# One core, one layer of RetNet + S5: tokens in natural order, modulation products with the weights stationary, and the S5 eigenvalues computed in the head

## The chip, the cores and the metric

The kernel runs on one core of one Trainium2 chip. The metric is the device time of one execution in microseconds (us), and the time before is the median of three runs. A core has five engines that each follow a queue of their own: TensorE (PE, with the weight loads counted apart as PEld), VectorE (DVE), ScalarE (ACT), GpSimd (POOL) and SyncE (SP), which here only issues DMA transfers; sixteen DMA engines carry these.

## The reference

One layer of a decoder over a prompt of 2048 tokens and eight short sample sequences (8 x 8 tokens), with 1024 channels, all in float32. Nine rows of conditioning `c` (one for the prompt, eight for the samples) become six modulation vectors each:

```
mod = silu(c) @ w_ada + b_ada                       # 9 x 6144
sh1, sc1, gt1, sh2, sc2, gt2 = split(mod, 6)
h = rms_norm(x, norm1_g) * (1 + sc1) + sh1
q, k, v, g, u, gate_r, gate_s = split(h @ w_in, ...)
q, k = rotary(q, pos), rotary(k, pos) * 128**-0.5
ret = rms_normalize(retention(q, k, v)) * silu(g)   # 4 heads, chunks of 128
lam_bar = exp((lam_re + i lam_im) * exp(log_dt))    # 32 groups x 64 states
b_bar = (lam_bar - 1) / lam * b
ssm = gelu(s5(u, lam_bar, b_bar, c, d))             # a linear recurrence over tokens
ssm = ssm * sigmoid(ssm @ w_glu)
merged = sigmoid(gate_r) * (ret @ w_br) + sigmoid(gate_s) * (ssm @ w_bs)
x = x + gt1 * (merged @ w_out)
h2 = rms_norm(x, norm2_g) * (1 + sc2) + sh2
x = x + gt2 * (square(relu(h2 @ w_up)) @ w_down)
y = rms_norm(x, norm_f_g)
```

The last states of the retention and of S5 are outputs too.

## The kernel before

**Stages.** A head (`setup`) prepares the modulation that the first normalization needs, and the first 512 rows of x. Then four super-blocks of 512 prompt tokens each (`super_block`, b = 0 to 3; b = 1 carries the sample tokens with it) run the mixer, and `feed_forward` runs the MLP and stores the rows of y.

**Products.** A dense product is split in three: an operand is written as a rounded part (hi, type fp32r) and the rest (lo), and hi*hi, hi*lo and lo*hi are summed in PSUM. Weights come in units of 128 x 2 x 512 float32 (512 KB): SyncE loads `wraw` (`fetch`, L181), ScalarE copies out `whi` (L191), and GpSimd, or VectorE for some names, subtracts to get `wlo` (L194, in `refill`). Four raw units and five split ones are buffered; `plan` fixes the order of the whole stream. A block (`block`, L253) takes four units (u, q, k, v, g, the four gate halves gr0, gs0, gr1, gs1, and wo0, wo1) or two (glu, br, bs). For each unit PE runs four groups of six products with 512 columns, one group for each of four PSUM banks. The results in the banks are evacuated behind the last unit: u by ScalarE (`ue`, L1528, which reorders tokens for S5 and is stored to DRAM), q and k by VectorE with the rotary factors (`rt`, L1555 to L1557), v by VectorE, g and the gates by ScalarE.

**Fillers.** Everything else is a generator (a filler): S5, retention, the norm of the next super-block, the output. `tick`, called once behind each group of six products, counts the fillers down and lets those due issue their next step, up to their next `yield n`. So the place of a filler's instructions in each engine's queue is set by the numbers in its `yield`s and by the delay it was spawned with; `finish(f)` issues the rest of one. Scheduling is otherwise the program's order, in which the compiler moves instructions a little.

**Modulation.** The 6144 columns of `w_ada` are twelve blocks of 512. Blocks 0 to 3 (sh1 and sc1) are computed in the head: `wa` holds a block as two halves of 1 MB, eight in all, and each block is eight float32 products in which the nine conditioning rows `z` are stationary and 512 weight columns move (L849), giving 9 x 512. Blocks 4 to 11 lie in super-block 0, one behind each of its first eight dense blocks (`more_ada`): their weights are in the ring's stream like any other (`names` "ada4" to "ada11", whose lo part is always VectorE's), and sixteen products with 512 columns (L259) give hi and lo sums in rows 0 to 8 and 32 to 40, which `ada`'s `evac` adds to the bias (L906, L907). In both cases the 9 x 512 sum is transposed back by four small PE products (L887 in the head, L913 later) into `modT`, 128 channels x 48 x 9. Blocks 4, 5, 10 and 11 also go to DRAM as rows (`modd`), where gt1 and gt2 are read across tokens.

**S5 setup.** `s5_setup` is a generator: loads of lam, dt, b, c, d; the eigenvalue part (L982 to L1077: expm1, sine and cosine by polynomials, all on 128 x 32 or 128 x 64 elements, on VectorE); powers by doubling (L1099 on); and sixteen groups of products that fold b and c with the powers into tables in DRAM (`s5bx`, `pw` L1155, `pk` L1156, `s5c`). It is spawned before u of super-block 0, and `finish(s5)` before v issues what is left of it; S5 proper (`s5`) runs beside v and g.

**Rows of tokens.** Inside each 128 tokens the kernel works in the order tau(r) = 8 (r mod 16) + r div 16. `x_rows` (L1450) loads rows with a pattern of three levels for that, the stores of y (L529 and `output_rows`) write with the same one, and the constants (causal mask, decay, rotary tables) follow it. S5 works on eight phases of the token index: with this order the eight phases of 16 tokens lie in runs of 16, which `ue` and `gw` (L1627) move as runs.

The functions that the change touches, with the lines as the profile numbers them:

Of the kernel before, what the change touches and what calls it, by code (L numbers as in the profile page):

```python
# [10 lines left out]
F32 = mybir.dt.float32  # L11
# [29 lines left out]
def _constants():  # L41
# [7 lines left out]
    tau = 8 * (r % 16) + r // 16  # L49
# [19 lines left out]
    pos = np.arange(SB)  # L69
    tok = 128 * (pos // 128) + 8 * (pos % 16) + pos % 128 // 16  # L70
# [12 lines left out]
class Layer:  # L83
# [79 lines left out]
    def plan(self, names, sides):  # L163
        self.names = list(names)
        self.stream = []
        for n, queue in zip(names, sides):
            for v in self.views(n):
                self.stream.append((n, v))
                if queue and n[:2] not in ("ad", "wo"):
                    self.stream.append(queue.pop(0))  # L170
# [5 lines left out]
        self.at = 0  # L176
# [8 lines left out]
    def refill(self, keep=False):  # L185
        nc = self.nc
        if self.split < len(self.stream):
# [5 lines left out]
            eng = nc.vector if name == "ad" or name in SIDE and self.split % 4 < 2 else nc.gpsimd  # L193
# [41 lines left out]
    def block(self, name, kind, src, evac=None, sample=None, order="k"):  # L235
# [5 lines left out]
        banks = [self.pd.tile([P, 512], F32, tag="pd", name=f"pd_{name}") for _ in range(4)] if kind else []  # L241
# [20 lines left out]
        if order == "k":  # L262
            for u in range(nu):
                w = self.weight(name)
                for j in range(4 if kind else 0):
# [7 lines left out]
                if sample:  # L273
                    for kk in range(2):
                        sample_products(2 * u + kk, w, kk)
                    if u == nu - 1:
                        self.spawn(sample[1](sb))
                    if kind is None:
                        self.refills()
                        self.tick()  # L280
                self.due += 1
                self.side()
            return
# [193 lines left out]
    def turn_back(self, k, g, i, accs):  # L477
# [44 lines left out]
        for t in range(4):  # L522
            for n in range(4):
# [5 lines left out]
                nc.sync.dma_start(raw_ap(self.o[0], P * (t0 + t) * D + 256 * n, [[D, 8], [8 * D, 16], [1, 256]]), o)  # L529

    def output_rows(self):
# [6 lines left out]
        for t in range(10):  # L538
# [3 lines left out]
            if t > 1:  # L542
# [3 lines left out]
                nc.sync.dma_start(raw_ap(self.o[0], P * (t - 2) * D, [[D, 8], [8 * D, 16], [1, D]]), o)  # L546
# [134 lines left out]
    def norm_out(self, pt, q, s, b, hh, hl, j, eng):  # L681
        nc = self.nc
        m = self.work("m", [P, 4, P])
        for a in range(4):
            k = 4 * q + a
            if eng is nc.vector:
                nc.scalar.activation(m[:, a], pt[:, a], AF.Identity, scale=s[:, k:k + 1], bias=b[:, k:k + 1])
            else:
                nc.vector.tensor_scalar(m[:, a], pt[:, a], s[:, k:k + 1], b[:, k:k + 1], op0=ALU.mult, op1=ALU.add)
# [82 lines left out]
    def setup(self):  # L772
# [24 lines left out]
        self.gT = cst.tile([P, 2, 8], F32, name="gT")  # L797
        self.R = cst.tile([P, H, P], F32, name="R")
        self.rk = cst.tile([P, 8], F32, name="rk")
        self.cT = cst.tile([P, 8, 41], F32R, name="cT")  # L800
        gn = self.work("gn", [16, P])
        dma(gn[0:8], i["norm1_g"].rearrange("o (k p) -> (o k) p", p=P))
        dma(gn[8:16], i["norm2_g"].rearrange("o (k p) -> (o k) p", p=P))
# [8 lines left out]
        ba = self.unit("ba", shape=(9, 2048))  # L812
        load(0)
        self.x_rows(xu[0][:, 0], 0, 0)
        dma(ba, raw_ap(i["b_ada"], 0, [[0, 9], [1, 2048]]))
        self.x_rows(xu[0][:, 1], 0, 1)
        load(2)
        for j in range(2, 4):
            self.x_rows(xu[1][:, j - 2], 0, j)
        load(1)  # L820
        load(3)
        for _ in range(RAW):
# [5 lines left out]
        V.tensor_scalar(th, th, 0.5, None, op0=ALU.mult)  # L828
# [3 lines left out]
        pg = self.bank("pg", [P, 16])  # L832
        nc.tensor.transpose(pg, gn, self.ident[:16, :16])
        z = self.unit("z", shape=(P, 8, 41))
        V.memset(z, 0.0)
        V.tensor_copy(self.cT, z)
        V.tensor_copy(z[:, :, 0:9], pt)
        nc.scalar.activation(self.cT[:, :, 0:9], z[:, :, 0:9], AF.Copy)
        V.tensor_sub(self.cT[:, :, 32:41], z[:, :, 0:9], self.cT[:, :, 0:9])
        V.tensor_copy(self.gT.rearrange("p a k -> p (a k)"), pg)  # L840
# [3 lines left out]
        x = [xu[j // 2][:, j % 2] for j in range(4)]  # L844

        def ada(n):
            pa = self.pd.tile([P, 512], F32, tag="pd", name=f"ps_ada{n}")
            for k in range(8):
                nc.tensor.matmul(pa[:9], z[:, k, 0:9], wa[2 * n + k // 4][:, k % 4], start=(k == 0), stop=(k == 7))  # L849
            self.mod_out(n, pa[0:9], ba[:, 512 * n:512 * n + 512])  # L850
# [8 lines left out]
        for q in range(2):  # L859
            ada(q)  # L860
            if q == 0:
                for j in range(4):
                    r = self.now(self.row_rstd(x[j]))
                    V.tensor_scalar(x[j], x[j], r, None, op0=ALU.mult)
                pts = [turn(q, j) for j in range(4)]
            else:
                for _ in range(2):
                    self.refill(True)
            ada(2 + q)
            self.scales(2 + q)  # L870
            for j in range(4):
                pt = turn(q, j) if q else pts[j]
                self.norm_out(pt, q, self.s1[:, :, 0], self.modT[:, 0:8, 0], self.hh, self.hl, j, nc.gpsimd)
        for _ in range(RING - 2):
            self.refill(True)
        self.late_setup = self.s5_setup()
        next(self.late_setup)

    def mod_out(self, n, p, bias):
        nc = self.nc  # L880
        t = self.work("mt", [9, 512])
        nc.vector.tensor_add(t, p, bias)
        if n in (4, 5, 10, 11):
            nc.sync.dma_start(self.modd[:, 512 * n:512 * n + 512], t)
        pt = self.pd.tile([P, 4, 9], F32, tag="pd", name="ptm")
        for a in range(4):
            nc.tensor.transpose(pt[:, a], t[:, a * P:a * P + P], self.ident[:9, :9])  # L887
# [944 lines left out]
```

## Time and profile before

| | |
|---|---|
| median of three runs | 3103.24 us (3094.15 to 3113.18) |
| the profiled execution's own time | 3099.62 us |
| its span in the trace | 3097.8 us |
| mean granted TensorE clock | 0.967 of full speed |
| busy: PE, PEld | 2911.6 us (94%), 2378.3 us (77%) |
| busy: DVE, ACT, POOL | 1822.8 us (59%), 1407.0 us (45%), 1720.4 us (56%) |
| moved by DMA | 518.62 MB, a mean of 167 GB/s |

Times in the trace count from the span's start. A group "L253 PE MATMUL pd_u<-hh,whi 128\*128 128x512" is line 253's products from `hh` and `whi` into bank `pd_u`, the stationary operand's shape ahead of the moving one's; "xN" is the number of records and the figure after the time is the duration, or the mean. A float32 product leaves two records. "idle <-X" names what released the engine. PE's ends are modelled, and the clock is the share of full speed granted by the throttle in that stretch.

### The profile page before, as it was taken

The page shows a single profiled execution, that of the slowest core. Times are in us where ns is not written, and L with a number is a line of the kernel's source. Part 1 is how long each engine was busy: PE and PEld are TensorE (multiplying, and loading weights), DVE is VectorE, ACT ScalarE, POOL GpSimd, SP SyncE. Part 2 cuts the span into 40 slices and gives each one's busy share as a digit, 9 for nine tenths or more (in the row PEclk, how much of TensorE's full clock was granted, in tenths as well). Part 3 has the DMA queues.
Part 4 walks back from the last instruction along what each step waited for, and adds up shares of the span by engine and source line. Part 5 has one row for each costly group of instructions (what it writes and reads, how often), then busy time and mean ns, then how long its engine had stood idle before and what let it go on. Part 6 is the DMA issues. An engine that isn't in the chain of part 4 may idle for free. (4 is left out here: it accounts for less than half of the span.)

```text
span 3097.8 us, 37373 instructions
## 1 busy us (share of the span) xinstructions
PE 2911.6 (94%) x13436; PEld 2378.3 (77%) x13436; DVE 1822.8 (59%) x2937; ACT 1407.0 (45%) x2296; POOL 1720.4 (56%) x1036
## 2 busy tenths in 40 slices
PE   7789999999999899999999989999999999998996
PEld 3567787788777778877788778887888788877875
DVE  5978644770575786365842545555556755554655
ACT  2233463322353334534234345566655555566743
POOL 2331464435253644655445477668777666688771
PEclk9889999999999999999999999999999999999998
DMA  8466445643236954447544455556545544466532
GB/s 231 156 192 209 132 128 165 185 110 119 80 92 191 277 181 121 141 137 245 190 133 151 148 191 180 187 197 204 186 154 171 193 168 155 150 220 225 182 128 96
DMA packets 336749, 518.62 MB, mean 167 GB/s; under 512 B 71462, under 2 KB 168246, under 8 KB 332459
## 3 DMA queue, kind: packets, MB, share of 16 engines
q1 hardware_dynamic: 336564, 516.23, 52.6%
q8 instruction: 106, 1.74, 0.2%
q14 instruction: 79, 0.65, 0.1%
HBM read 401.39 MB, written 114.78 MB: 167 GB/s over the span
## 5 line engine op out<-in xcount | busy, mean ns | idle before, releaser
L194 POOL TENSOR_TENSOR wlo<-wraw,whi 128x1024 fp32r<-128x1024 f32 x248 | 616.8, 2498 | 729.0 <-ACT whi L191 585.7
L409 PE MATMUL pq_down<-shi,tw 128*128 128x512 f32 x1792 | 565.5, 395 | 20.7 <-DVE acc L469 10.2
L191 ACT ACTIVATE whi<-wraw 128x1024 fp32r<-128x1024 f32 x312 | 324.4, 1058 | 571.2 <-PE pd_wo L253 63.7
L409 PE MATMUL pq_up<-shi,tw 128*128 128x512 f32 x1792 | 556.9, 391 | 11.9 <-ACT tw L310 8.0
L409 PEld LDWEIGHTS pq_down<-shi,tw 128*128 128x128 f32 x1792 | 340.2, 190 | 96.1 <-ACT acc L467 10.4
L409 PEld LDWEIGHTS pq_up<-shi,tw 128*128 128x128 f32 x1792 | 337.6, 188 | 84.9 <-ACT tw L310 9.2
L311 POOL TENSOR_TENSOR tw<-traw,tw 128x512 fp32r<-128x512 f32 x192 | 274.4, 1442 | 144.7 <-ACT tw L310 144.4
L409 PE MATMUL pq_down<-slo,tw 128*128 128x512 f32 x896 | 353.1, 394 | 0.9 <-DVE slo L382 0.9
L409 PE MATMUL pq_up<-slo,tw 128*128 128x512 f32 x896 | 349.7, 391 | 0.0
L396 ACT ACTIVATE shi<-sw 128x1024 fp32r<-128x1024 f32 x140 | 147.0, 1057 | 167.4 <-DMA sw<-sd 107.9
L469 DVE SCALAR_TENSOR_TENSOR acc<-pq_down,modT,acc 128x512 f32<-128x512 f32 x224 | 161.9, 745 | 95.3 <-PE pq_down L409 95.0
L409 PEld LDWEIGHTS pq_down<-slo,tw 128*128 128x128 f32 x896 | 170.5, 190 | 36.0 <-DVE slo L382 1.4
L409 PEld LDWEIGHTS pq_up<-slo,tw 128*128 128x128 f32 x896 | 168.9, 189 | 34.5
L382 DVE TENSOR_TENSOR slo<-sw,far 128x512 fp32r<-128x512 f32 x160 | 103.7, 682 | 113.3 <-ACT far L381 99.6
L310 ACT ACTIVATE tw<-traw 128x512 fp32r<-128x512 f32 x224 | 137.4, 624 | 54.7 <-PE pq_down L409 39.1
L401 DVE TENSOR_TENSOR slo<-sw,shi 128x1024 fp32r<-128x1024 f32 x60 | 117.7, 1976 | 71.8 <-ACT shi L396 70.6
L419 ACT ACTIVATE aq<-pq_up 128x512 f32<-128x512 f32 x128 | 72.6, 592 | 170.7 <-PE pq_up L409 170.7
L194 DVE TENSOR_TENSOR wlo<-wraw,whi 128x1024 fp32r<-128x1024 f32 x64 | 88.3, 1380 | 73.0 <-ACT whi L191 68.6
L345 POOL TENSOR_TENSOR ts<-traw,ts 128x512 f32<-128x512 f32 x64 | 95.2, 1487 | 53.9 <-issue 49.2
L253 PE MATMUL pd_wo<-whi,mh 128*128 128x512 f32 x256 | 103.9, 410 | 18.9 <-DVE tw L1718 18.9
L310 ACT ACTIVATE tw<-ts 128x512 fp32r<-128x512 f32 x128 | 80.2, 627 | 81.2 <-PE pq_up L409 71.9
L311 POOL TENSOR_TENSOR tw<-t,tw 128x512 fp32r<-128x512 f32 x64 | 88.4, 1387 | 50.2 <-ACT tw L310 50.2
(537 smaller groups left out, 6865.4 us busy)
## 6 DMA issues: line engine op xcount, KB each, us to landing
wraw<-in_w_in_dram SPq DMA_DIRECT2D x144, 512.0 KB
sw<-sd SPq DMA_DIRECT2D x112, 512.0 KB
s5p<-s5c SPq DMA_DIRECT2D x32, 1024.0 KB
traw<-in_w_up_dram SPq DMA_DIRECT2D x64, 512.0 KB
sd<-sq SPq DMA_DIRECT2D x32, 1024.0 KB
sd<-aq SPq DMA_DIRECT2D x32, 768.0 KB
traw<-in_w_down_dram SPq DMA_DIRECT2D x24, 1024.0 KB
wraw<-in_w_ada_dram SPq DMA_DIRECT2D x32, 512.0 KB
```

The costliest lines, as they stand in the source:

```text
L191: a = nc.scalar.activation(hi, raw, AF.Copy)
L194: l = eng.tensor_sub(lo, raw, hi)
L253: nc.tensor.matmul(banks[j], a, b, start=(k == 0 and z == 0), stop=(k == nk - 1 and z == 2))
L310: self.nc.scalar.activation(t[:, 0], x, AF.Copy)
L311: eng.tensor_sub(t[:, 1], x, t[:, 0])
L345: G.tensor_sub(x[p], l, x[m] if isinstance(m, int) else m)
L382: self.nc.vector.tensor_sub(d, a, c)
L396: nc.scalar.activation(hi[:, a], t, AF.Copy)
L401: V.tensor_sub(lo[:, a], t, hi[:, a])
L409: self.nc.tensor.matmul(bank, w, x, start=(first and a == 0 and z == 0), stop=(a == 3 and z == 2), skip_group_check=True)
L419: copy = lambda d, b: nc.scalar.activation(d, b, AF.Copy)
L469: V.scalar_tensor_tensor(d, b, g, d, op0=ALU.mult, op1=ALU.add)
```

## The change

Three things change.

*Token order.* Tokens keep their natural order inside 128 rows. Loads and stores of rows become plain two-level patterns; the constants follow; the reorder for S5 in `ue` and `gw` now reads or writes every eighth element.

*Modulation.* In all twelve blocks the weights become the stationary operand, 128 x 128 float32 at a time, and the nine columns of `z` move, so the sums come out with the channels across partitions, where `modT` wants them. In the head that makes 128 small products in place of 32. Bias and gains are loaded as 64 rows and transposed once (`bg`). Blocks 4 to 11 leave the ring's stream: `ada_fetch` loads one unit of raw weights into a buffer of two (`wada`), and `ada_side`, called behind each unit of a dense block of super-block 0 (32 times), asks for the next unit, issues eight small products and spawns the one addition that folds them into `modT`. Only blocks 4, 5, 10 and 11 are transposed back (`pr`) for `modd`. `norm_out` scales on ScalarE always, and so does the head's `norm`.

*S5 setup.* The eigenvalue part runs in the head, in four pieces (`next(s5)`); the loads of b, c, d and the transposes of c come later; the pauses between the steps change; `first_s5` chains the remainder with S5 proper, which is finished behind gr0 instead of before retention. Retention of super-block 0 therefore begins behind gr0, not before it.

The order of instructions on PE in the head, up to the first products of u (one row for a run of like instructions; `pt` are transposes of x and of the conditioning, `ptm` those of the sums). Before:

```order
L831 MATMUL pt<-cpk,th 128x9 x8
L833 MATMUL pg<-cpk,gn 128x16
L849 MATMUL ps_ada_176<-wa,z 9x512 x8
L887 MATMUL ptm<-cpk,mt 128x9 x4
L849 MATMUL ps_ada_285<-wa,z 9x512 x8
L856 MATMUL pt<-cpk,x_125 128x128 x8
L887 MATMUL ptm<-cpk,mt 128x9 x4
L849 MATMUL ps_ada_332<-wa,z 9x512 x8
L856 MATMUL pt<-cpk,x_126 128x128 x8
```

Afterwards (`pl` are the transposes of lam for S5):

```order
L829 MATMUL pt<-cpk,th 128x9 x8
L831 MATMUL pg<-cpk,gb 128x64
L843 MATMUL ps_ada<-z,wa 128x9 x32
L982 MATMUL pl<-cpk,lam 128x32 x2
L862 MATMUL pt<-cpk,x_126 128x128 x4
L843 MATMUL ps_ada<-z,wa 128x9 x2
L862 MATMUL pt<-cpk,x_126 128x128 x4
L843 MATMUL ps_ada<-z,wa 128x9 x60
L862 MATMUL pt<-cpk,x_127 128x128 x4
```

Each block's eight wide products became thirty-two narrow ones, the `ptm` transposes are gone, and two for S5 have come in.

The order on PE behind u in super-block 0. Before, one modulation block stands between the last products of u and the first of q:

```order
L253 MATMUL pd_u<-hh,wlo 128x512
L259 MATMUL ps_ada_816<-whi,cT 41x512
L259 MATMUL ps_ada_816<-wlo,cT 41x512
L259 MATMUL ps_ada_816<-whi,cT 41x512
L259 MATMUL ps_ada_816<-wlo,cT 41x512
L259 MATMUL ps_ada_816<-whi,cT 41x512
```

Afterwards, a burst of eight stands among the products of u, behind its first unit:

```order
L252 MATMUL pd_u<-hh,wlo 128x512
L252 MATMUL pd_u<-hh,whi 128x512 x4
L918 MATMUL ps_ada<-z,wada 128x9 x8
L252 MATMUL pd_u<-hl,whi 128x512 x4
L252 MATMUL pd_u<-hh,wlo 128x512
```

The sixteen products in a row are replaced by bursts of eight, each behind one unit of a dense block.

The order on VectorE at the end of the head. Before, the eigenvalue steps (`s5w`) stand behind the last modulation sum:

```order
L888 COPY modT<-ptm 128x36
L894 TENSOR_SCALAR s_108<-modT 128x36
L895 TENSOR_TENSOR s_108<-s_108,gT 128x36
L689 TENSOR_SCALAR m<-pt,s_108,modT 128x128 x16
L982 TENSOR_SCALAR s5w<-s5w 128x32
L983 TENSOR_SCALAR s5w<-s5w 128x32
```

Afterwards they stand ahead of the second modulation sum of the head (block 2's), up to line 1068:

```order
L1067 TENSOR_TENSOR s5w<-s5w 128x32
L1068 TENSOR_SCALAR s5w<-s5w 64x32
L849 TENSOR_TENSOR modT<-ps_ada,bg 128x36
L850 TENSOR_TENSOR modT<-modT,ps_ada 128x36
L946 TENSOR_SCALAR s_108<-modT 128x36
L947 TENSOR_TENSOR s_108<-s_108,bg 128x36
```

The scalings of x by `norm_out` (L689) have left VectorE's queue.

The diff, cut to its core:

```diff
-    tau = 8 * (r % 16) + r // 16
+    tau = r
...
-    tok = 128 * (pos // 128) + 8 * (pos % 16) + pos % 128 // 16
+    tok = np.arange(SB)
...
                 self.due += 1
                 self.side()
+                self.ada_side()
...
-                nc.sync.dma_start(raw_ap(self.o[0], P * (t0 + t) * D + 256 * n, [[D, 8], [8 * D, 16], [1, 256]]), o)
+                nc.sync.dma_start(raw_ap(self.o[0], P * (t0 + t) * D + 256 * n, [[D, P], [1, 256]]), o)
...
-                nc.tensor.matmul(pa[:9], z[:, k, 0:9], wa[2 * n + k // 4][:, k % 4], ...)
+        def products(n):
+            pa = self.pd.tile([P, 2, 4, 9], F32, tag="pd", name="ps_ada")
+            for h in range(2):
+                for a in range(4):
+                    for k in range(4):
+                        nc.tensor.matmul(pa[:, h, a], wa[2 * n + h][:, k, a * P:a * P + P], z[:, 4 * h + k],
+                                         start=(k == 0), stop=(k == 3))
+        def sums(n, pa):
+            m = self.modT[:, 4 * n:4 * n + 4]
+            V.tensor_add(m, pa[:, 0], self.bT[:, 4 * n:4 * n + 4, None].to_broadcast([P, 4, 9]))
+            V.tensor_add(m, m, pa[:, 1])
...
+        pa = products(0)
+        norm(0)
+        sums(0, pa)
+        next(s5)
+        norm(1)
+        pts = [turn(0, 0), turn(0, 1)]
+        pa = products(2)
+        sums(2, pa)
...
+    def ada_fetch(self, at):
+        if at < 32:
+            self.nc.sync.dma_start(self.ada_w[:, at % 2], self.ada_todo[at][2])
+    def ada_side(self):
...
+        w = self.ada_w[:, at % 2]
+        self.ada_fetch(at + 1)
+        p = self.bank("ps_ada", [P, 4, 9])
+        for a in range(4):
+            for k in range(2):
+                nc.tensor.matmul(p[:, a], w[:, k, a * P:a * P + P], self.z[:, 2 * u + k], ...)
+        def evac():
+            yield 1
+            nc.vector.tensor_add(m, p, m if u else self.bT[...])
...
-    def ada(self, n):
...
+    def first_s5(self):
+        yield from self.late_setup
+        yield 6
+        yield from self.s5(0, 4)
...
-            nc.scalar.activation(t.rearrange("p (s n c) -> p n s c", s=8, n=4),
-                                 p.rearrange("p (n s c) -> p n s c", s=8, n=4), AF.Copy)
+            nc.scalar.activation(t.rearrange("p (s c) -> p s c", s=8), p.rearrange("p (c s) -> p s c", s=8), AF.Copy)
...
-    src = raw_ap(self.i["x_prompt"], (b * SB + P * j) * D, [[D, 8], [8 * D, 16], [1, D]])
+    src = raw_ap(self.i["x_prompt"], (b * SB + P * j) * D, [[D, P], [1, D]])
...
-        if b == 0:
-            self.finish(s5)
-            s5 = self.spawn(self.s5(b, 4), 13)
...
             self.block(n, "T", srcT(hh, hl), ev_gate(n), S(hS, ev_gS(a)))
-            more_ada()
+            if not b and a == 0:
+                self.finish(s5)
+                rh, rl = begin()
```

More of the change, by code (lines that the diff above doesn't have):

```diff
@@ L168, in plan @@
                 self.stream.append((n, v))
-                if queue and n[:2] not in ("ad", "wo"):
+                if queue and n[:2] != "wo":
                     self.stream.append(queue.pop(0))
@@ L192, in refill @@
             name = self.stream[self.split][0][:2]
-            eng = nc.vector if name == "ad" or name in SIDE and self.split % 4 < 2 else nc.gpsimd
+            eng = nc.vector if name in SIDE and self.split % 4 < 2 else nc.gpsimd
             l = eng.tensor_sub(lo, raw, hi)
@@ L264, in block @@
                 w = self.weight(name)
-                for j in range(4 if kind else 0):
+                for j in range(4):
                     for kk in range(2):
@@ L857, in turn, with out @@
             return pt
[L859 to L873, printed above, removed]
+        def out(pt, q, j):
+            self.norm_out(pt, q, self.s1[:, :, 0], self.modT[:, 0:8, 0], self.hh, self.hl, j, nc.gpsimd)
@@ new lines, in setup @@
+        pa = products(0)
+        norm(0)
+        sums(0, pa)
+        next(s5)
+        norm(1)
+        pts = [turn(0, 0), turn(0, 1)]
+        pa = products(2)
+        sums(2, pa)
+        for j in range(2):
+            out(pts[j], 0, j)
+        next(s5)
+        for j in range(2, 4):
+            norm(j)
+        for j in range(2, 4):
+            out(turn(0, j), 0, j)
+        for _ in range(2):
+            self.refill(True)
+        next(s5)
+        pa = products(1)
+        sums(1, pa)
@@ L874, in setup @@
+        pts = [turn(1, j) for j in range(4)]
+        pa = products(3)
+        sums(3, pa)
+        for j in range(4):
+            out(pts[j], 1, j)
         for _ in range(RING - 2):
             self.refill(True)
-        self.late_setup = self.s5_setup()
-        next(self.late_setup)
-    def mod_out(self, n, p, bias):
-        nc = self.nc
[L881 to L885, printed above, removed]
-        for a in range(4):
-            nc.tensor.transpose(pt[:, a], t[:, a * P:a * P + P], self.ident[:9, :9])
-        nc.vector.tensor_copy(self.modT[:, 4 * n:4 * n + 4], pt)
+        next(s5)
@@ L1476, in run @@
         names, sides = [], []
-        late = iter(range(4, 12))
         for b in range(NSB):
-            main = []
-            for n in ("u", "q", "k", "v", "g", "gr0", "gs0", "gr1", "gs1"):
-                main.append(n)
-                if b == 0 and n != "gs1":
-                    main.append(f"ada{next(late)}")
+            main = ["u", "q", "k", "v", "g", "gr0", "gs0", "gr1", "gs1"]
             main += ["glu", "br0", "br1", "bs0", "bs1", "wo0", "wo1"]
@@ L1494, in run @@
         self.setup()
-        late = iter(range(4, 12))
         for b in range(NSB):
-            self.super_block(b, late)
+            self.super_block(b)
         self.finish(*self.fillers)
```

199 lines of the change are left out of this document (96 added, 103 removed).

## The prediction

> **What bounds the kernel now.** I read the page first, then busy time by stage (columns after the length: busy us and instructions of PE, PEld, DVE, ACT, POOL; then PE's granted clock, the DMA share, GB/s), then who PE waits for.
>
> ```profile
> PE 2911.6 (94%) x13436; PEld 2378.3 (77%) x13436; DVE 1822.8 (59%) x2937; ACT 1407.0 (45%) x2296; POOL 1720.4 (56%) x1036
> ```
>
> ```profile
> 0.00:57.90 57.90, 39.32 (x121) 11.69 (x121) 21.44 (x76) 12.36 (x25) 10.29 (x10) 0.94 0.86 256
> 57.90:85.20 27.30, 27.30 (x124) 20.85 (x123) 26.52 (x95) 13.81 (x19) 12.31 (x7) 1.00 0.78 183
> 85.20:163.80 78.60, 60.46 (x269) 46.71 (x269) 77.33 (x171) 21.18 (x23) 29.92 (x15) 0.87 0.44 137
> 163.80:205.20 41.40, 29.41 (x129) 23.51 (x128) 40.26 (x54) 9.78 (x16) 14.89 (x8) 0.90 0.64 215
> 205.20:214.90 9.70, 9.33 (x48) 9.23 (x48) 5.49 (x13) 2.39 (x4) 0.00 (x0) 0.50 0.32 129
> 214.90:310.20 95.30, 89.36 (x494) 74.01 (x495) 74.67 (x171) 31.94 (x52) 18.89 (x8) 0.95 0.70 212
> 310.20:516.50 206.30, 199.29 (x922) 160.12 (x921) 113.02 (x184) 95.77 (x156) 101.64 (x49) 0.97 0.44 135
> ```
>
> ```profile
> PE pd_k L253 <- DVE rt L1556: 10.2, 1, 10.2
> PE pw L1155 <- DVE s5bx L1148: 8.0, 1, 8.0
> PE pt L913 <- DVE mt L907: 7.9, 1, 7.9
> PE pd_v L253 <- DVE rt L1556: 3.7, 1, 3.7
> ```
>
> PE is the bound: 94% of the span. The head lasts until 57.9 us, super-block 0 from there to 516.5 (458.6 us). Only in the head and in super-block 0 does another engine set the pace: from 57.9 to 205.2 VectorE is busy 144.1 of 147.3 us, and PE's four longest waits there, 29.8 us together, are on VectorE. The waits also cost clock: 0.87, 0.90 and 0.50. The compiled order of super-blocks 1 to 3 is nearly the old one and that of the feed-forward part is the old one on PE, so the sum is made over the head, super-block 0, and the loads and stores of token rows.
>
> **The head: S5 eigenvalues.** Inside super-block 0 these small VectorE operations meet ScalarE and GpSimd at work; in the head GpSimd does nothing until 42 us.
>
> ```profile
> 84.58 2.43 DVE L1032 TENSOR_SCALAR s5w<-s5w 128x64 f32<-128x64 f32 x1
> ...
> 94.08 0.18 DVE L1032 TENSOR_SCALAR s5w<-s5w 128x64 f32<-128x64 f32 x1
> ```
>
> ```profile
> 82.74 11.34 POOL L194 TENSOR_TENSOR wlo<-wraw,whi 128x1024 fp32r<-128x1024 f32 x4 [12.00 <-ACT whi L191]
> ```
>
> The same operation costs 0.18 us alone and 2.43 us while GpSimd runs a split. Some 130 of them leave super-block 0; at 0.18 they are 23 us in the head, on an engine that has 36 us free there (57.9 - 21.44). They stand ahead of the second modulation sum in VectorE's queue, but need PE only for one early pair of transposes, and PE will be later than they (next part): nothing on the path. If PE were quick there, they would hold that sum back a few us. The head's 32 scalings of x move from VectorE to ScalarE (busy 12.36 of 57.9 us): the last 16 and their copies, estimated at 0.3 to 0.6 us each from ue's 0.6 us for 512 columns (below), take 7 to 12 us, and PE spends 11 us on the first half of u meanwhile (48 products at 0.23): nothing.
>
> **The head: modulation products.** Before, 32 float32 products with 512 moving columns, two records each; afterwards 128 with 9 moving columns and a float32 block of 128x128 to be loaded for each. The nearest rows to these are the S5 products with 16 moving columns, at both clocks, and those with 64.
>
> ```profile
> 9.90 8.53 PE L849 MATMUL ps_ada<-wa,z 128*9 128x512 f32 x16 [1.25 <-DVE z L837]
> 24.56 9.73 PE L849 MATMUL ps_ada<-wa,z 128*9 128x512 f32 x16 [4.95 <-DMA wa<-in_w_ada_dram]
> 34.22 1.41 PE L856 MATMUL pt<-cpk,x 128*128 128x128 f32 x8
> 49.77 7.04 PE L849 MATMUL ps_ada<-wa,z 128*9 128x512 f32 x16
> ...
> 192.19 0.96 PE L1156 MATMUL pk<-s5bc,s5bx 128*128 128x16 f32 x8
> 210.36 1.73 PE L1156 MATMUL pk<-s5bc,s5bx 128*128 128x16 f32 x8
> 211.93 1.09 PE L1155 MATMUL pw<-cpk,s5bx 128*128 128x128 f32 x4
> ```
>
> ```profile
> 1503.89 0.33 PE L1242 MATMUL py<-s5t,s5p 128*128 128x64 f32 x2
> ...
> 1505.40 0.39 PE L1241 MATMUL py<-s5u,s5p 128*128 128x64 f32 x2
> 1505.91 0.39 PE L253 MATMUL pd_v<-whi,hl 128*128 128x512 f32 x1
> ```
>
> At full clock seven py products take 1.51 us (1503.89 to 1505.40), 0.22 each, and four pk at most 0.96, 0.24 each: I take 0.22; the columns hardly enter. At half clock four pk take 1.57 us (210.36 to 211.93), 0.39 each, a transpose at most 0.27 (1.09 / 4). Which clock will it be? From 205.2 to 214.9 PE was busy 9.33 of 9.70 us and PEld 9.23, with these small products, and the clock stayed at 0.50 throughout. A stream of 9 columns is thinner still, so I take half clock for the whole head: 128 x 0.39 = 50 us and 32 transposes x 0.25 = 8, from 9.9: PE reaches u at 68, not 57.9: **+10**. A lower bound: the 48 records from 205.2 to 214.9 are 16 pairs of a transpose and a pk, 0.61 a pair, so 0.36 for pk, and u at 63: +5. u then begins cold; the product that began cold took 9.73 us against 7.04, so **+3**. Weights are no limit: eight tiles of 1 MB, four x tiles and two weight pieces of half a MB, 11.5 MB, land at 50 us even at the head's 256 GB/s of now, ahead of the last 32 products.
>
> [...]
>
> **Super-block 0, what goes.** The eight late modulation blocks of 16 products, their transposes and their VectorE work:
>
> ```profile
> 81.58 0.39 PE L259 MATMUL ps_ada<-whi,cT 128*41 128x512 f32 x1
> 85.25 0.40 PE L253 MATMUL pd_q<-hh,whi 128*128 128x512 f32 x1
> ```
>
> ```profile
> L194 DVE TENSOR_TENSOR wlo<-wraw,whi 128x1024 fp32r<-128x1024 f32 x32 | 42.2, 1318 | 21.2 <-ACT whi L191 21.2
> L913 PE MATMUL pt<-cpk,mt 9*128 9x9 f32 x32 | 3.6, 214 | 7.9 <-DVE mt L907 7.9
> ```
>
> PE gives back 8 x 3.67 (81.58 to 85.25) = 29.4 us and 3.6 of transposes. VectorE loses 42 us of splits and the eigenvalues, and gains 32 small additions, so it no longer fills 57.9 to 205.2: the 29.8 us of waits go, and with them the lost clock, 60.46 x 0.13 + 29.41 x 0.10 + 9.33 x 0.50 = 15.5. Together **-78.3**.
>
> **Super-block 0, what comes.** 256 products with 9 columns in bursts of eight. Between dense products the clock stays full (the dense product at 1505.91, behind the py run, takes 0.39, the full-clock duration), so 256 x 0.22 = 56.3 us, all on PE's path (at 0.24: 61). Sixteen transposes at 0.18 (34.22): 2.8. What is late next: PE itself, and S5's chain on VectorE, which now lies in gr0 and gs0; I leave 8 us of waits (0 to 20). In seven places of the order bursts stand beside S5 or retention products, so that 4 to 7 us pass without a dense product; such a run can lose the clock as at 205.2, 2.7 us each: five of seven, 13.5 (0 to 19). Together **+80.6**. The block ends **+2**: its PE work grew by what its waits shrank. Retention begins a gate block later and still has three blocks to lie beside.
>
> **Token rows.** The old strided patterns run at half the DMA engines. At the end, where nothing else runs:
>
> ```profile
> 3085.00:3090.00 5.00, 0.00 (x0) 0.00 (x0) 0.00 (x0) 0.00 (x0) 0.00 (x0) 0.50 0.54 190
> ```
>
> ```profile
> 3071.49 22.51 SPq L529 DMA_DIRECT2D out_dram<-acc  x32
> 80.65 0.37 SPq L181 DMA_DIRECT2D wraw<-in_w_in_dram  x1
> ```
>
> Share 0.54 at 190 GB/s; the plain weight loads reach a share of 0.86 with these mixed in. 32 stores leave SyncE 0.70 us apart, a plain one is issued in 0.37. The last 16 wait for a norm that is ready at 3080.6; at 0.45 each they are out at 3088 and land at 3090, not 3097.8. Between -2 (issue stays at 0.6) and -8 I take **-6**. The 28 row loads and 8 stores elsewhere are hidden but share the engines with weights: **-3** (0 to -6).
>
> In exchange the reordering for S5 now reads or writes every eighth element:
>
> ```profile
> L1528 ACT ACTIVATE ue<-pd_u x16: 577/602/639, 79.9 to 1414.0; 128x512 f32<-128x512 f32 x16
> ```
>
> ```profile
> 95.20 0.17 DVE L1062 COPY cs<-s5w 128x32 f32<-128x32 f32 x1
> ...
> 107.01 0.20 DVE L1099 COPY s5pw<-s5pw 128x32 f32<-128x32 f32 x1
> ```
>
> VectorE copies every eighth of 32 elements (L1099) in 0.20 us, contiguous ones (L1062) in 0.17. I take 0 for the 32 ScalarE operations; at twice the time, +0.6 each, only the four before q and the four before glu are near the path: 5 us a super-block at the most, 20 in all if nothing covered them. [...]
>
> **The sum.** +10 +3 +2 -6 -3 = +6 us, against the profiled execution's own 3099.62 (span 3097.8): 3105.6. The median of the runs is 3103.24, 3.6 us above that execution, so I forecast 3109 as a median, 0.2% up. Its own range, with the terms at their bounds and taken as independent (root of the squares): downwards 5 (head), 8 (waits), 13.5 (clock), 2 and 3 (rows) make 17; upwards 12 (waits), 5.5 (clock), 5 (products), 4 and 3 (rows) and 10 (half of the strided copies) make 18: 3092 to 3127.
>
> **Rivals.** [...] 14%.
>
> *PE waits for the late weights.* The late modulation weights now come in a two-slot buffer straight to PE, asked for one quarter block (7 us) ahead, in SyncE's queue behind loads, S5 tables and ue stores that wait for others. Now ScalarE meets them, nine pieces ahead of use:
>
> ```profile
> ACT whi L191 <- DMA wraw<-in_w_ada_dram: 24.1, 9, 9.4
> ```
>
> If those nine waits fell on PE: +24, and five cold starts, 13.5: 3146, slower by 1.4%. Behind such a wait stand the block's dense products, and behind those the evacuations of u, q, k, v. It decides where a load takes over 7 us from its turn. For it: DMA share 0.78 in u, and S5's small loads. Against: 0.44 to 0.64 from q on. 14%.
>
> *Every burst drops the clock.* 32 x 2.7 = 86, less 13.5: 3182. The py burst of the same length did not. 4%.
>
> *The change saves no PE work and no waits matter* (VectorE's relief comes to nothing, as the waits move to S5's steps in gr0): the 29.8 and 15.5 stay, less the 8 left above, +37: 3146. Against: the 42 us of splits and the eigenvalues that leave. 6%.
>
> **How the numbers follow.** Likeliest 62%. 1% is 31 us and about what a measurement of this kernel tells from no change. Below 3072: most of the first rival's 14%, less what falls just short: 0.09. Above 3134: the other rivals, 24%, of which some fall short, and little of the likeliest: 0.18. Within: 0.73. The range takes in half of the first rival and most of the second: 3076 to 3146.
>
> **What would show it.** Right: u's first product at 63 to 70 us with the clock at 0.5 before it; ps_ada records at about 0.2 us a record in the head and 0.11 later; no wait of PE on rt between 85 and 205; super-block 1 beginning near 530; the last store landing 20 us after PE's end. Wrong: u beginning before 50 (the first rival), PE waits on wada (the second), ps_ada followed by dense products 0.43 us apart (the third), ue over 1 us.

## The result

The changed kernel takes 3067.43 us (median of four runs, 3065.49 to 3075.05). The kernel before, run beside it, takes 3101.14. The ratio is 0.9882, with a 95% interval of 0.9856 to 0.9908: 1.2% faster. The forecast was 3109 us with a range of 3076 to 3146, so the time lies outside the range and on the other side of no change.

The head and super-block 0 went as forecast. On the timeline of TensorE in the changed kernel (start, length, line, tiles, count), u begins at 66.84 us; the forecast said 68. The small products take 13.79 us for 64 records, two a product, 0.43 us each:

```profile
8.71 13.79 PE L843 MATMUL ps_ada<-z,wa 128*128 128x9 f32 x64 [0.70 <-DMA wa<-in_w_ada_dram]
...
25.29 25.61 PE L843 MATMUL ps_ada<-z,wa 128*128 128x9 f32 x120
...
66.84 0.77 PE L252 MATMUL pd_u<-hh,whi 128*128 128x512 f32 x1
```

Super-block 1 begins at 530.8, and "near 530" was the forecast. Everything behind that was forecast 9 us shorter and is 45 us shorter. The table gives the lengths of the stages in the two profiled executions, and in two experiments told of below. A stage ends where the next one's first product starts; the last two columns are split at TensorE's last product. Executions of the same instructions differ by 2 or 3 us in most stages, and by 7 in super-block 2, which took 401.4 and 402.7 us in two runs and 408.7 and 409.3 in two others whose edits lie outside it.

| us | head | super-block 0 | 1 | 2 | 3 | feed-forward | tail |
|---|---|---|---|---|---|---|---|
| before | 57.9 | 458.5 | 458.3 | 412.8 | 404.0 | 1281.1 | 25.1 |
| changed | 66.8 | 463.9 | 445.9 | 401.4 | 400.9 | 1269.4 | 18.6 |
| token order alone | 47.1 | 454.7 | 449.8 | 402.8 | 400.8 | 1272.7 | 18.9 |
| the other two alone | 70.8 | 467.3 | 457.2 | 409.8 | 408.7 | 1279.7 | 25.3 |

Busy time hides this. The page's first line says that TensorE is now busy longer, not less:

```profile
PE 2949.6 (96%) x13980; PEld 2467.9 (80%) x13980; DVE 1741.1 (57%) x2873; ACT 1395.4 (45%) x2295; POOL 1723.8 (56%) x1036
```

The waits of TensorE from super-block 1 on say where to look. Of the kernel before, from 516 to 1790 us (waiting tile and who is waited for, total, times, longest), the first row is the one that matters:

```profile
PE pd_wo L253 <- DVE tw L1718: 16.2, 4, 6.4
```

In the changed kernel it is

```profile
PE pd_wo L252 <- DVE tw L1739: 2.4, 1, 2.4
```

Block wo's banks are emptied by VectorE's `tw`, the product of the sum and gt1. In super-block 1 of the kernel before, the timelines of SyncE and VectorE show the load of gt1 issued behind the four loads of x, and the first `tw` 19.7 us later:

```profile
924.00 2.68 SPq L1450 DMA_DIRECT2D x<-in_x_prompt_dram  x4
926.73 0.49 SPq L926 DMA_DIRECT2D gt<-modd  x1
```

```profile
946.44 0.69 DVE L1718 SCALAR_TENSOR_TENSOR tw<-pd_wo,gt 128x512 f32<-128x512 f32 x1 [16.64 <-DMA gt<-modd]
```

In the changed kernel the order of the loads is the same, and 8.2 us pass:

```profile
935.18 0.63 SPq L954 DMA_DIRECT2D gt<-modd  x1
```

```profile
943.39 0.69 DVE L1739 SCALAR_TENSOR_TENSOR tw<-pd_wo,gt 128x512 f32<-128x512 f32 x1 [4.34 <-DMA gt<-modd]
```

The busy time by stretches (last three columns: granted clock, DMA share, GB/s) shows why. Where little but the old pattern's rows is under way (936 to 944 us), the mean busy share of the DMA engines is 0.51 to 0.52, and 131 to 132 GB/s move; with the plain pattern the share reaches 1.03, and 411 GB/s move. Before, then after:

```profile
936.00:940.00 4.00, 4.00 (x20) 3.30 (x19) 0.00 (x0) 0.73 (x1) 0.00 (x0) 1.00 0.52 131
```

```profile
937.00:941.00 4.00, 4.00 (x13) 3.21 (x14) 0.69 (x1) 0.60 (x1) 0.00 (x0) 0.57 1.03 411
```

The slowest dimension of the old pattern has 8 entries, that of the plain one 128. Why the one is carried at half the share of the other isn't shown.

For block wo of super-block 1 as a whole (before, then after), 7.2 us went and the mean clock rose from 0.92 to 0.97: the waits had cost clock too.

```profile
909.40:974.80 65.40, 55.42 (x230) 44.93 (x230) 31.84 (x33) 14.44 (x20) 22.06 (x11) 0.92 0.45 131
```

```profile
918.50:976.70 58.20, 53.20 (x231) 43.53 (x229) 33.57 (x33) 14.36 (x20) 23.07 (x11) 0.97 0.44 146
```

The tail was forecast 6 us shorter and is 6.5 shorter. The 32 stores leave SyncE in 17.44 us, not 22.51, and the last norm, ready at 3056.23, is followed by 10.7 us, not 17.2:

```profile
3047.12 17.44 SPq L526 DMA_DIRECT2D out_dram<-acc  x32
...
3056.23 3.30 ACT L525 ACTIVATE acc<-acc,y 128x256 f32<-128x256 f32 x8 [3.55 <-DVE y L631]
```

### The profile page after: what moved, and what is told of

It reads as the page before. It is cut to its first block, busy times and chain, and to the rows that moved or that the text cites. A ratio compares the mean times of both kernels' runs of the same rounds, so it can differ in the third digit from the quotient of the medians.

```text
span 3067.0 us, 38337 instructions
## 1 busy us (share of the span) xinstructions
PE 2949.6 (96%) x13980; PEld 2467.9 (80%) x13980; DVE 1741.1 (57%) x2873; ACT 1395.4 (45%) x2295; POOL 1723.8 (56%) x1036
## 4 chain that ended last, share of the span: by engine, by line
PE 75%; DVE 12%; DMA 5%; ACT 3%; issue 2%; POOL 2%; SPq 1%; ACTq 0%; DVEq 0%; POOLq 0%
PE pq_up L406 17%; PE pq_down L406 14%; PE pd_gr L252 6%; PE pd_gs L252 5%; PE pd_wo L252 4%; PE pd_br L252 3%; PE pd_g L252 3%; PE pd_u L252 3%; DMA sw<-sd 2%; PE pd_k L252 2%; PE ps_ada L843 2%; PE pd_bs L252 2%; PE ps_ada L918 2%; PE pd_glu L252 2%; PE pd_q L252 1%
## 5 line engine op out<-in xcount | busy, mean ns | idle before, releaser
L406 PE MATMUL pq_up<-shi,tw 128*128 128x512 f32 x1792 | 557.1, 391 | 10.8 <-ACT tw L307 6.9
L190 ACT ACTIVATE whi<-wraw 128x1024 fp32r<-128x1024 f32 x280 | 291.9, 1060 | 564.5 <-issue 56.1
L307 ACT ACTIVATE tw<-ts 128x512 fp32r<-128x512 f32 x128 | 80.2, 627 | 80.9 <-PE pq_up L406 71.6
L342 POOL TENSOR_TENSOR ts<-traw 128x512 f32<-128x512 f32 x64 | 86.8, 1357 | 45.1 <-DMA traw<-in_w_up_dram 26.8
L444 DVE TENSOR_TENSOR sq<-aq 128x512 f32<-128x512 f32 x32 | 30.5, 952 | 131.4 <-ACT aq L421 131.4
```

The source lines that it names most:

```text
L190: a = nc.scalar.activation(hi, raw, AF.Copy)
L307: self.nc.scalar.activation(t[:, 0], x, AF.Copy)
L342: G.tensor_sub(x[p], l, x[m] if isinstance(m, int) else m)
L406: self.nc.tensor.matmul(bank, w, x, start=(first and a == 0 and z == 0), stop=(a == 3 and z == 2), skip_group_check=True)
```

## The experiments

All ratios are to the kernel before, run on the same chip, with their 95% intervals.

### Which part carries the gain

Token order alone, on the kernel before:

```diff
-    tau = 8 * (r % 16) + r // 16
+    tau = r
-    tok = 128 * (pos // 128) + 8 * (pos % 16) + pos % 128 // 16
+    tok = np.arange(SB)
-    ... [[D, 8], [8 * D, 16], [1, 256]] ...
+    ... [[D, P], [1, 256]] ...
-    ... [[D, 8], [8 * D, 16], [1, D]] ...
+    ... [[D, P], [1, D]] ...
-    ... "p (n s c) -> p n s c" ...
+    ... "p (c s) -> p s c" ...
```

> The kernel before with the token order alone changed: rows loaded and stored in natural order, the reorder for S5 at every eighth element; modulation and S5 setup as before. Theory A: the row transfers carry the whole gain, since the changed kernel is 45.1 us shorter from super-block 1 on (2536.2 against 2581.3 us) and 14.3 us longer up to there (530.8 against 516.5): head 57.9 as before, 3099.6 - 45 = about 3055 us, with gt1's wait in wo and the store tail shortened in all super-blocks. Theory B: as predicted, the rows are worth 9 us, and the later stages got shorter because of what the other two parts changed in the order: about 3090 us.

Measured: 3050.99 us, ratio 0.9826 (0.9809 to 0.9842). And the reverse, the changed kernel with these lines as they were:

> The changed kernel with the old token order put back (three-level row patterns, runs of 16 for S5), modulation and S5 setup as changed. Theory A (rows carry it all): 3067 + 45 = about 3112 us, slower than before; super-block 1 begins near 531, and the VectorE addition in wo waits for gt1 12 us or more again. Theory B (rows worth 9): about 3076 us.

Measured: 3114.49 us, ratio 1.0031 (1.0019 to 1.0043). Theory A holds in both: the token order is worth some 47 to 54 us, and the other two parts together cost 10 to 16 us. The run of the token order alone is even a little shorter than A said, because its head ends at 47.1 us, 10.8 us earlier: the strided rows had been ahead of `wa` in SyncE's queue, and TensorE's wait of 4.9 us for `wa` is gone. In the changed kernel TensorE is too slow in the head for more than 4.0 of these to count (66.8 against 70.8).

### Loads and stores apart

```diff
-        src = raw_ap(self.i["x_prompt"], (b * SB + P * j) * D, [[D, P], [1, D]])
+        src = raw_ap(self.i["x_prompt"], (b * SB + P * j) * D, [[D, 8], [8 * D, 16], [1, D]])
```

> The changed kernel with the three-level pattern put back in the loads of x rows alone; the rows then stand in another order than the constants assume, so that the output is not the reference's, while the work is the same. By stages of the run with all of the old order against the changed kernel, the loads should cost 4 us in the head and 3, 11, 8 and 8 in the four super-blocks, through the load of gt1 that stands behind four of them: 3067 + 35 = 3100 us. Rival: the stores carry the larger part, and the loads are hidden but for the head: 3071 us.

Measured: 3103.05 us, ratio 0.9988 (0.9971 to 1.0004): the strided loads alone take back 36 us. In its profile the four blocks wo are 36.7 us longer together than in the changed kernel, of 39.7 us for the whole span.

```diff
-    ... raw_ap(self.o[0], P * (t0 + t) * D + 256 * n, [[D, P], [1, 256]]) ...
+    ... raw_ap(self.o[0], P * (t0 + t) * D + 256 * n, [[D, 8], [8 * D, 16], [1, 256]]) ...
-    ... raw_ap(self.o[0], P * (t - 2) * D, [[D, P], [1, D]]) ...
+    ... raw_ap(self.o[0], P * (t - 2) * D, [[D, 8], [8 * D, 16], [1, D]]) ...
```

> The changed kernel with the three-level pattern put back in the stores of y alone (the output's rows are permuted within 128, the work is the same). By stages: 9 to 10 us in the feed-forward part where the first eight stores of y stand ahead of the loads of activations in SyncE's queue, and 6.5 us at the end: 3083 us. Rival: only the end is exposed, as predicted: 3073 us.

Measured: 3088.67 us (3078.28 to 3090.9), ratio 0.9925 (0.9899 to 0.9951): 21 us by the medians, 13 by the ratios. By the ratios, loads (33 us) and stores (13) add up to the 46 that both cost. The profiled execution is one of the two shortest of five. It is 11 us longer than the changed kernel's, with 6.0 us more in the feed-forward part and 6.7 in the tail. Why the other three take 9 to 11 us beyond that isn't explained. The place in the feed-forward part is the stretch where the first eight stores of y have gone out. The same products of `pq_down`, in the changed kernel and with the strided stores:

```profile
2791.00:2822.00 31.00, 31.00 (x138) 25.38 (x137) 16.70 (x26) 20.98 (x31) 30.71 (x24) 1.00 0.69 228
```

```profile
2791.00:2832.00 41.00, 33.58 (x139) 25.12 (x138) 20.39 (x32) 27.00 (x41) 36.22 (x28) 1.00 0.63 202
```

138 records took 31 us in the one and 139 took 41 in the other. TensorE's waits there, 9 us, are on VectorE (`acc`, 7.3 us, and `slo`) and ScalarE. ScalarE waits 13.9 us there for the loads (`sw`) that stand behind the stores in SyncE's queue, against 9.9 in the changed kernel's stretch; how TensorE's waits hang on these isn't shown.

### Is it the wait for gt1?

The kernel before, with the load of gt1 issued first:

```diff
-        for j in range(4):
-            self.x_rows(x1[j // 2][:, j % 2], b, j)
         gt1 = self.unit("gt", shape=(P, D))
         self.mod_row(gt1, 2)
+        for j in range(4):
+            self.x_rows(x1[j // 2][:, j % 2], b, j)
```

> The kernel before with one change: in each super-block the load of gt1 is issued ahead of the four strided loads of x, not behind them. Theory: what the loads cost in super-blocks 1 to 3 (12, 11 and 7 us) is the wait of the first product of wo's evacuation for gt1, which lands 19.7 us after its issue behind 2 MB that go at half the rate; ahead of them it lands in about 5, the evacuation waits only for the first rows of x, and 5 to 7 us a super-block come back: 3078 to 3090 us against 3104. Rival: the addition behind it needs x's rows, which land as late, and VectorE waits there instead: within 5 us of before.

Measured: 3087.23 us, ratio 0.9929 (0.9903 to 0.9955): 17 us, by moving one line. VectorE's timeline shows the first `tw` waiting for TensorE and no longer for gt1; the additions wait for x, 1.4 to 2.5 us at a time, which the buffers of `tw` cover for the most part:

```profile
931.29 0.69 DVE L1718 SCALAR_TENSOR_TENSOR tw<-pd_wo,gt 128x512 f32<-128x512 f32 x1 [2.82 <-PE pd_wo L253]
...
935.66 0.69 DVE L1719 TENSOR_TENSOR x<-x,tw 128x512 f32<-128x512 f32 x1 [1.43 <-DMA x<-in_x_prompt_dram]
```

So the place of gt1 in the queue makes about half of what the strided loads cost. The lengths of block wo in the four super-blocks show where:

| us in block wo | super-block 0 | 1 | 2 | 3 |
|---|---|---|---|---|
| before | 50.2 | 65.4 | 50.6 | 60.2 |
| before, gt1 first | 45.1 | 59.5 | 43.6 | 60.9 |
| token order alone | 45.0 | 59.4 | 43.6 | 54.4 |

In super-blocks 0 to 2 the place of gt1 makes all of what the strided rows cost there, 18 us. In super-block 3 it makes nothing. There the traces show another load behind the rows in SyncE's queue, that of activations for the feed-forward part (`sw`). ScalarE waits 11.5 us for it before, 9.6 with gt1 first and 3.7 with plain rows, and VectorE's `slo`, which needs ScalarE's result, stands ahead of `tw`. No run moves that load by itself.

### The other two parts, apart

The token order with the modulation, and the S5 setup scheduled as before (the `next(s5)` of the eigenvalue part leave the head, and the old order of loads, transposes and pauses inside `s5_setup` comes back):

```diff
-        next(s5)
...
-            s5 = self.spawn(self.first_s5(), 2)
+            s5 = self.spawn(self.late_setup, 2)
...
+        if b == 0:
+            self.finish(s5)
+            s5 = self.spawn(self.s5(b, 4), 13)
```

> The changed kernel with the S5 setup scheduled as before (eigenvalues inside super-block 0, S5 finished before v and before retention): token order and modulation alone. If the eigenvalue steps in the head relieve super-block 0, as predicted, it gets longer by the waits that come back, 10 to 30 us: 3077 to 3097 us. If VectorE's relief came from the splits that left with the old modulation alone, 3064 to 3070 us.

Measured: 3091.36 us, ratio 0.9951 (0.9937 to 0.9966). The token order with the S5 setup, and the modulation as before (the new `s5_setup`, `first_s5` and their places in the old kernel's head and in `super_block`):

> The kernel before with token order and S5 setup changed (eigenvalues in the head, S5 finished behind gr0), the modulation products as before. If the parts add, the S5 part is worth what its absence cost (3091.4 - 3067.4 = 24 us): 3051 - 24 = 3027 us. Rival: with the old modulation VectorE still has the 42 us of splits beside S5's tables and stays the bound of super-block 0, and in the head, now 47 us long, the eigenvalue steps hold up the sums that u waits for: 3040 to 3055 us.

Measured: 3061.76 us, ratio 0.9849 (0.9826 to 0.9871). The parts don't add. On top of the token order (3051), the modulation alone costs 40 us, the S5 setup alone 11 (7 by the ratios, whose intervals overlap), and the two together 16. With the eigenvalue steps still in super-block 0, this is 17 us longer than in the changed kernel (481.1 against 463.9), and TensorE's waits in it, most of them on VectorE, are 29.5 us against 17.8. The longest is at the transposes back, for the small addition behind a modulation burst. This is the first of TensorE's waits up to 560 us, with the S5 setup as before:

```profile
PE pr L927 <- DVE modT L918: 13.9, 1, 13.9
```

With the old modulation and the S5 setup in its new places, VectorE has both the tables of S5 and the splits, and k waits for the banks of q:

```profile
PE pd_k L252 <- DVE rt L1564: 23.0, 2, 20.1
```

The head is longer in that run, too: 58.8 us against 47.1, with waits on VectorE of 6.9 us ahead of the first products (1.2 without the eigenvalue part) and 6.5 us ahead of the transposes `ptm` (1.5 without). The first of these is a load: VectorE's first eigenvalue step waits 5.6 us for `log_dt`, and the copy of `z`, which the products need, stands behind it. The eigenvalue part is not free in a head of 47 us. In the changed kernel's it nearly is: u begins at 66.8 us with it, and at 66.1 without (the run of 3091.36 us).

The wait at the transposes back exists in the changed kernel as well (10.1 us, its longest in super-block 0), so it makes 4 of the 12 us of waits that the S5 setup took away:

```profile
PE pr L932 <- DVE modT L923: 10.1, 1, 10.1
```

Issued later:

```diff
             if n in (4, 5, 10, 11):
-                yield 2
+                yield 12
```

> The changed kernel with one number changed: the transposes of the late modulation sums back to rows are issued twelve steps behind the addition, not two. Theory: TensorE's 10.1 us wait at 113 to 123 is for a small addition that stands in VectorE's queue behind S5's tables, and goes, with part of the clock lost there (0.77 in q): 3050 to 3058 us. Rival: VectorE is the bound from 97 to 130 (busy 32.9 of 33 us), so the wait moves to the next product that needs VectorE, S5's or k's banks: 3063 to 3068.

Measured: 3068.31 us, ratio 0.9877 (0.9862 to 0.9892): no difference, as the rival said: the wait turns up as 7.4 us at S5's products, which need VectorE's tables. Super-block 0 is 6 us shorter in its profile, and super-block 2, which the edit doesn't touch, is 7 us longer.

```profile
PE pw L1182 <- DVE s5bx L1175: 7.4, 1, 7.4
```

### The clock and the small products

With 64 moving columns in place of 9:

```diff
-        self.z = z = cst.tile([P, 8, 9], F32, name="z")
+        z = cst.tile([P, 16, 9], F32, name="z")
+        self.z = zf = z.rearrange("p k c -> p (k c)")
...
-    ... z[:, 4 * h + k] ...
+    ... zf[:, 9 * (4 * h + k):9 * (4 * h + k) + 64] ...
```

> The changed kernel with 64 moving columns instead of 9 in all modulation products (the nine wanted ones and what lies behind them in memory; the sums use nine). Clock theory: 9 columns let the clock fall because the array is hardly in use, the weight load sets the pace of 0.22 us a product at full clock either way, and 64 columns keep it open: 128 products in the head at 0.22 and u at about 50 (the last weights land at 42), and most of the some 30 us of clock lost in super-block 0 come back: 3025 to 3040 us. Rival, the pace of 0.43 us in the head is the weight load's or the queue's own and not the clock's: u stays at 67 and the time at 3067. Third: 64 columns cost more than the load hides: head longer by 5 to 15 us, 3075 to 3085.

Measured: 3059.55 us, ratio 0.9847 (0.9833 to 0.9862). The head kept its pace (69.6 us), and super-block 0 became 14.6 us shorter. TensorE's waits in it hardly changed (17.8 and 19.1 us), and its mean granted clock rose from 0.92 to 0.97. That is half of the theory and half of the rival; what lets the clock fall with 9 columns isn't shown. The two come together if 64 columns keep an open clock open but don't open a closed one. To test that, five products with 512 columns of zeros ahead of the first transposes:

```diff
+        wu = self.pd.tile([P, 512], F32, tag="pd", name="warm")
+        for _ in range(4):
+            nc.tensor.matmul(wu, self.R[:, 0], self.R.rearrange("p h n -> p (h n)"), start=True, stop=True)
...
+        nc.tensor.matmul(wu, self.R[:, 0], self.R.rearrange("p h n -> p (h n)"), start=True, stop=True)
```

> The kernel with 64 moving columns, and five products with 512 columns of zeros ahead of the first transposes, while TensorE waits for the conditioning (their result is used by nothing). Theory: 64 columns at half clock are too little to open the clock (0.43 us a product in the head), but enough to keep it open: behind the five products the 128 take 0.22 each, u begins at 44 to 50, and the time is 3059.6 - 22 = 3037 us, give or take 6. Rival: the pace of 0.43 in the head is not the clock's: u at 70 or later and 3060 us. Third: the clock closes again in the gaps before the first products: no gain, 3060 us, with the first few products at 0.22.

Measured: 3056.62 us, ratio 0.9835 (0.9807 to 0.9864), u at 54.8. The same 64 records, first without and then with the five products:

```profile
8.38 13.89 PE L845 MATMUL ps_ada<-z,wa 128*128 128x64 f32 x64 [0.34 <-DVE bg L835]
```

```profile
9.70 7.36 PE L849 MATMUL ps_ada<-z,wa 128*128 128x64 f32 x64
...
28.99 10.08 PE L849 MATMUL ps_ada<-z,wa 128*128 128x64 f32 x46 [3.30 <-DMA wa<-in_w_ada_dram]
```

0.43 us a product became 0.23. Behind a wait of 3.3 us for weights the clock was closed (0.50), and the next 23 products took 0.44 each again. The stretches show the granted clock in both states:

```profile
9.70:17.00 7.30, 7.30 (x65) 7.23 (x65) 3.41 (x27) 2.67 (x8) 0.00 (x0) 1.00 0.99 351
...
29.00:38.80 9.80, 9.80 (x46) 9.80 (x47) 5.88 (x33) 7.09 (x16) 2.50 (x2) 0.50 1.07 370
```

So the head's pace is the clock's.

What goes ahead of the clock's opening at the end of the head is not a run of small products but the transposes of x among them. In the changed kernel the granted clock changes for the first time at 56.4 us, and the products behind that take 0.24 us each, until it closes again at 59.8:

```profile
53.20 2.80 PE L862 MATMUL pt<-cpk,x 128*128 128x128 f32 x12
...
57.36 0.96 PE L843 MATMUL ps_ada<-z,wa 128*128 128x9 f32 x8
```

The twelve transposes, with 128 moving columns, end 0.4 us ahead of it. With 64 columns the clock opens at 68.7 us, behind the twelve transposes that end at 68.1, and in the run with the five products it opens again at 48.0, behind those that end at 47.0. No run varies the transposes, so that they open the clock isn't shown, nor which of their properties would.

Of the 14.8 us by which the five products made the head shorter, super-block 0 gave 4.5 back; the intervals of the two runs overlap, so over the whole run the gain isn't shown.

The run without the five products issued the small ones back to back from 25 to 61 us at the pace of half clock, 0.43 us each: 36 us of a queue that was never empty did not open the clock.

### A faster kernel

Old products in the head (nine columns stationary, 512 moving, four transposes a block), 64 columns in the late bursts:

```diff
+                nc.tensor.matmul(pa[:9], z[:, k], wa[2 * n + k // 4][:, k % 4], start=(k == 0), stop=(k == 7))
...
+                nc.tensor.transpose(ptm[:, a], t[:, a * P:a * P + P], self.ident[:9, :9])
```

> The kernel with 64 moving columns in the late modulation bursts, and in the head the old form of the products (nine columns stationary, 512 weight columns moving, four transposes a block). Theory: the head's small products at half clock are what costs in the head; with the wide ones u begins at 47 to 52, as with the token order alone, in place of 69.6, and the rest goes as with 64 columns: 3059.6 - 20 = 3037 to 3043 us. Rival: the head is held by something else that the change brought in, the eigenvalue steps in VectorE's queue or the later loads of wa: u at 60 or later, 3050 us and more.

Measured: 3043.37 us, ratio 0.9797 (0.978 to 0.9814), the fastest of all, 24 us below the changed kernel. u begins at 51.7. Against the token order alone (3050.99) it is 8 us, and the two intervals just overlap. Adding gt1 first and the later transposes:

> The kernel with the old head products and 64 columns in the late bursts, with gt1's load ahead of the x rows and the transposes back issued twelve steps behind the addition. gt1 still costs 4.3 and 3.2 us on VectorE in super-blocks 1 and 2 but hardly TensorE: 0 to 2 us each. The later transposes take away 7.2 us of TensorE's waiting in super-block 0, of which S5's products may wait for the greater part. 3033 to 3043 us.

Measured: 3046.03 us, ratio 0.9799 (0.9777 to 0.982): no difference. With plain rows, neither is on the path.

## Why the prediction was wrong, point by point

**The failed step: "Token rows".** The row loads and the eight early stores were called hidden and priced at -3 (0 to -6). Measured by stages, with the other two parts held (the second row of the table against the fourth), they are worth 4.0 in the head, 3.4, 11.3, 8.4 and 7.8 in the super-blocks and 10.3 in the feed-forward part: 45 us. Of the 31 us in the super-blocks, 28 lie in block wo, where loads of 512 KB stand behind the strided rows in SyncE's queue and VectorE waits for them, directly or through ScalarE. What was read for the tail, half of the DMA engines by a share of 0.54 at 190 GB/s, was right as a share (0.80 at 267 GB/s with plain rows, 3058 to 3062 us of the changed kernel), and so was its price (-6, measured -6.5). It was not carried to the other places where the same patterns stand ahead of something that is waited for. The trace of before had it: `pd_wo` waiting for `tw` is the largest wait from super-block 1 on. The prediction listed waits from 57.9 to 205.2 us alone, having decided from busy time that nothing else sets the pace behind, and from there the word "hidden" had no row under it.

**The head: right.** Half clock, 0.39 us a product from the S5 rows, u at 68; measured 0.43 and 66.8. Eigenvalue steps at nothing: right for this head. (The lower bound given for u, 63, is 64 by its own terms, 9.9 + 46 + 8.) By the pace of the products (0.43 us each) the clock was at half until 56.4 us, and it was again from 59.8 into u, where it opened at 70.0. What the step missed is that the head's other term, the old order of x rows, was holding the old head back by 10.8 us. The true price of the new head is 19.7 us (66.8 against 47.1).

**Super-block 0: right in its sum.** +5 with the cold start, measured +5.4. Of the terms, waits: forecast 22 us fewer (29.8 gone, 8 left). TensorE's waits in the whole block went from 43.4 to 17.8 us, 26 fewer, though 10.1 of those left are at the transposes back, which the prediction did not have, and 2.9 on `rt` at k, which it had excluded. Small products at 0.22: measured 0.21 (eight in the 1.70 us up to the next dense product). Clock: 15.5 us won back and 13.5 lost were forecast, and the block's mean granted clock stayed nearly the same (0.93 before, 0.92 afterwards). In block q it fell to 0.77, part of it in the wait of 10.1 us. With 64 columns super-block 0 gains 14.6 us. A burst in u, and block q as a stretch:

```profile
80.23 1.85 PE L918 MATMUL ps_ada<-z,wada 128*128 128x9 f32 x16
81.93 1.19 PE L252 MATMUL pd_u<-hl,whi 128*128 128x512 f32 x4
```

```profile
97.10:149.00 51.90, 41.79 (x197) 36.09 (x196) 37.43 (x64) 7.48 (x10) 16.68 (x5) 0.77 0.52 171
```

**Strided reordering: for `gw` the upper bound was the value, and it is nearly hidden.** `gw` takes twice the time, before and after:

```profile
L1630 ACT ACTIVATE gw<-yl x16: 612/619/623, 400.6 to 1675.2; 128x512 f32<-128x512 f32 x16
```

```profile
L1652 ACT ACTIVATE gw<-yl x16: 1127/1202/1217, 418.5 to 1669.1; 128x512 f32<-128x512 f32 x16
```

It writes every eighth element of SBUF, in 1.20 us against 0.62 for runs of 16. `ue`, which reads every eighth of PSUM, takes what it took (0.60 us). Why the one takes longer and the other doesn't isn't shown. TensorE waits 1.4 us in all for `gh`, which is made from `gw`.

**Rivals.** For the first rival's 14% (u before 50) no run shows a head of small products that keeps the clock open: in the changed kernel's it was open for 3.4 us only (56.4 to 59.8), and u began at 66.8. TensorE never waited for `wada`, and bursts did not drop the clock each time (the granted clock is 1.00 from 80.2 to 83.0 us, through the one at 80.23). The relief of VectorE did not come to nothing: the waits in super-block 0 fell by 26 us, and without the S5 part the kernel takes 24 us more.

## What to carry to other kernels

Before a transfer is called hidden, list who waits behind it: what stands in its queue after it, and whose first instruction needs that. Read the waits of every stage, also where the bound engine is 96% busy, since four waits of 16 us together show in no share of a span of 3000. Where one pattern is slow, go through all its uses and not only the one that lies bare at the end.

A part that saves nothing on its path can still be needed by another part, or spoil it: the three parts here are worth -54 us (token order), and on top of that +40 (modulation) and +11 (S5 setup) singly, and +16 together, and the best kernel keeps two of them whole and half of the third. What that kernel has beyond the token order is worth 8 us.

## What was unexpected of the hardware

Small float32 products with 64 moving columns ran 0.43 us each from a closed clock for as long as they lasted (36 us without a gap), and 0.23 from an open one; behind a wait of 3.3 us it was closed again. With 9 columns in place of 64, the clock was also closed for longer among dense products (super-block 0: a mean of 0.92 against 0.97, and 463.9 against 449.3 us).

In the changed kernel's trace the clock column of a stretch is no evidence ahead of the clock's first change (56.4 us): it reads 1.00 over the first 50 us, where 64 records take 13.79 us and the pace of the products, 0.43 us against 0.24 behind the change, says half clock:

```profile
8.70:22.40 13.70, 13.69 (x64) 13.70 (x64) 5.32 (x40) 4.96 (x10) 0.00 (x0) 1.00 1.02 383
```

Read the clock there by the time of a product that is known at both clocks.
